# Two hybrid encoder layers on one core: cross attention in a written order, the rotation's tables at its end, state products from split operands, later transposes of x

## The chip, the core and the metric

The kernel runs on one core of one Trainium2 chip, as a single launch. The time is the device time of that launch in microseconds (us). Three runs of the kernel before took 2188.62, 2189.69 and 2190.12 us; the median, 2189.69 us, is the time that the change is compared with. One further execution was profiled; the profile shows when each instruction of each engine ran and what it waited for.

The engines carry these names: PE is TensorE (matrix products and transposes), PEld its loading of weights, DVE is VectorE, ACT is ScalarE, POOL is GpSimd, and SP is the queue of SyncE, from which all of this kernel's transfers are issued. An `L99` in a row of the profile is line 99 of the kernel; since most operations go through small helpers, many rows carry a helper's line, and the tile's name tells them apart.

## The reference

Two layers work on a residual stream x of 512 tokens and 1024 channels. Each layer has three branches on the same x, whose outputs are gated, summed, projected and normalised. All is float32.

- Branch A is a bidirectional state-space scan (SSD) with 4 groups g of 8 heads. A depthwise convolution over 5 tokens and SiLU make xs, B and C. The sequence is cut into 4 chunks of 128 tokens. For each group, chunk and direction there is a state: `states = einsum('bcqgn,bgrcq,bcqgrp->bcgrpn', bm, decay_states, xs)`, a product of B (128 tokens by 128) with the x of 8 heads (128 tokens by 512), weighted by a decay and by dt. Each state decays into the next chunk.
- Branch B is differential attention with rotary position, so it needs tables of cos and sin of position times frequency.
- Branch C is cross attention with 4 heads of 256 into 256 memory tokens: `s = q mk / 16; p = softmax(s); o = p mv`, and `y = o * silu(gate)`. The keys and values come from `mem @ w_mem_kv`, per layer.

Each branch is projected to 1024 channels and multiplied by a sigmoid gate computed from x.

## The kernel before

**Split products.** TensorE's fast float format (`F32R`) keeps fewer bits, so most operands are kept as a pair: `split(h, l, x)` writes h as a rounded copy (one instruction on ACT) and l = x - h (one subtraction on DVE, which needs h). `mm3` then does three matrix products: l by h, h by l, h by h. A plain `mm` on float32 tiles has no split.

**Units.** All weights come in units of 128 by 1024. A unit is loaded by a transfer (`wr`, 2 buffers), split (`wh`, `wl`, 3 buffers each; ACT and DVE), and used by one projection: 24 matrix products of 512 columns against xh and xl, into one of three PSUM banks `pj`. `emit` keeps loads and splits two units ahead of the unit that the plan has reached. The units for the memory's keys and values have 24 products of 256 columns.

**The plan.** `self.T(fn, unit)` appends to a plan; `emit` runs it in order and so gives every instruction a rank. A planner then orders each engine's instructions: it takes what is ready by its own costs, earliest rank first. Within `manual_schedule(engines={PE})` the order of TensorE alone is the written one; DVE, ACT and SP are still ordered by the planner. Each engine and each queue works through its list strictly in that order. `late(n)` changes the rank of what it encloses: with `-LN` the work counts as 300 places earlier.

**SSD stage (`ssd`).** TensorE's order is written out with `U` (a unit, and jobs placed between its two halves) and `J` (a job of its own). For group g there are the units B (`bu`), C (`cu`), four of x (`xu`), four of z (`zu`); `xturn(g, b)` transposes block b of x on TensorE once the convolution (ACT, four DVE steps `acc`, ACT into `xsC`) is done; `bturn` transposes B into `bT`. `expos(g, b)` loads decays by broadcast (`ab`, `eb`), clips them on DVE and exponentiates them on ACT into `m`. `block(g, b)` does the group's output for block b and reads `m` and the states `prev`. `states(g, part)` weights x on DVE (`xw`, line 518), multiplies `bT` by it on TensorE with a plain float32 `mm`, and adds the result to `prev`, for one chunk of each direction; there are 3 parts per group. `wu` projects the previous group, `gu` is one of 12 gate units, used to fill, whose result `tg` (2 buffers) goes to DRAM as `dgt` and is read back later.

**Cross stage (`cross`).** At its begin, in layer 0, the memory is loaded and split into `mhl` and `rope_tables` computes cos and sin with some 40 DVE steps in tiles `cw`. Then follow, head by head, q units (`qpart`), key units with a trip of the keys through DRAM (`mo`, `dkv`, `mkv`), gate units with the output of the head before (`opart`), the head's scores, softmax and transposes (`att`), and value units. The order of TensorE is the planner's here. In layer 1 the keys and values are made earlier, inside `wout` of layer 0. `branch_out` projects the branch.

Of the kernel before, what the change touches and what calls it, by code (L numbers as in the profile page):

```python
# [12 lines left out]
F32R = mybir.dt.float32r  # L13
# [38 lines left out]
class Net:  # L52
# [73 lines left out]

    def emit(self, look_raw=2, look=2):
# [110 lines left out]
    def rope_tables(self, sp, tag):  # L238
# [4 lines left out]
        t0, t1 = (self.t(sp, [P, 4, S], tag) for _ in range(2))  # L243
# [200 lines left out]
    def ssd(self, l):  # L444
# [66 lines left out]

        def states(g, part):

            sp = self.sp
            for d, c in ((0, part), (1, 3 - part)):
# [165 lines left out]
        def U(unit, *amid):  # L681
            gen, u = unit

            def f(wh, wl):
                g = gen(wh, wl)
                next(g, None)
                for fn, *args in amid:
                    fn(*args)
                next(g, None)
            self.T(f, u)  # L690

        def J(fn, *args):
            self.T(lambda: fn(*args))
# [50 lines left out]
        J(expos, 0, 0)  # L744
        U(gu())
        J(states, 0, 0)
        U(zu(0, 0), (states, 0, 1))
        for g in range(1, 4):
            p = g - 1
            U(bu(g))  # L750
            if g == 1:
                J(states, 0, 2)
# [6 lines left out]
            U(gu())  # L759
            J(block, p, 1)  # L760
            U(xu(g, 0), (bturn, g))
# [83 lines left out]
    def cross(self, l):  # L845
        nc = self.nc

        def begin():
            self.cp_ctx = ExitStack()
            cp = self.crp = self.cp_ctx.enter_context(self.tc.tile_pool(name="crossp", bufs=2, reuse_waits="tile"))  # L850
            if load is not None:
                load(cp, raw="cpp")
                self.rope_tables(cp, "cw")
# [3 lines left out]
        def fetch(i, h):  # L857
            def f():
                t = self.mkv[i] = self.t(self.crp, [P, 2, 2, M], f"mkv{i}", F32R)
# [3 lines left out]
        def qpart(h, i):  # L863
            def f(wh, wl):
                if i == 0:
                    self.cq = self.t(self.crp, [P, 2, 2, S], "cq", F32R)
                ps = self.proj(wh, wl)
                self.split(self.cq[:, 0, i, :], self.cq[:, 1, i, :], ps)
            return f

        def att(h):
            def f():
                cp = self.crp
                cq, mk = self.cq, self.mkv[0]
                cw = self.cw[h] = self.t(cp, [P, 2, 2, S], "cw", F32R)
                for qp in range(2):
                    ps = self.bank(self.pm, "pm")
                    for i in range(2):
                        q = slice((2 * qp + i) * P, (2 * qp + i + 1) * P)
                        for k in range(2):  # L880
                            self.mm3(ps[:, i * M:(i + 1) * M], cq[:, 0, k, q], cq[:, 1, k, q],
                                     mk[:, k, 0, :], mk[:, k, 1, :], k == 0, k == 1)
                    mx = self.t(cp, [P, 2], "cmx")
                    sm = self.t(cp, [P, 2], "csm")
                    psv = ps.rearrange("p (i m) -> p i m", i=2)
                    nc.vector.reduce_max(out=mx, in_=psv, axis=AX.X)
                    self.ts(mx, mx, -1.0 / 16.0, ALU.mult)
                    p = self.t(cp, [P, 2, M], "cpp")
                    for i in range(2):
                        self.act(p[:, i, :], psv[:, i, :], AF.Exp, scale=1.0 / 16.0, bias=mx[:, i:i + 1],  # L890
                                 accum_out=sm[:, i:i + 1])
                    nc.vector.reciprocal(out=sm, in_=sm)
                    for i in range(2):
                        self.ts(p[:, i, :], p[:, i, :], sm[:, i:i + 1], ALU.mult, 0.5, ALU.mult)
                    pt = self.bank(self.pt, "pt")
                    for k in range(2):
                        for i in range(2):
                            self.tr(pt[:, (2 * k + i) * P:(2 * k + i + 1) * P], p[:, i, k * P:(k + 1) * P])
                    q = slice(2 * qp * P, 2 * (qp + 1) * P)
                    self.split(cw[:, 0, :, q], cw[:, 1, :, q], pt.rearrange("p (k q) -> p k q", k=2))  # L900
            return f

        def opart(h, i):
            def f(wh, wl):
                cp, mv = self.crp, self.mkv[1]
                j = 2 * h + i
                ps = self.proj(wh, wl)
                th = self.t(cp, [P, S], "cth")
                self.act(th, ps, AF.Tanh, scale=0.5)
                self.stt(th, th, 1.0, ps, ALU.add, ALU.mult)  # L910
                po = self.bank(self.pm, "pm")
                for k in range(2):
                    e = slice(k * P, (k + 1) * P)
                    self.mm3(po, mv[:, i, 0, e], mv[:, i, 1, e], self.cw[h][:, 0, k, :], self.cw[h][:, 1, k, :],
                             k == 0, k == 1)
                self.tt(th, th, po, ALU.mult)
                self.split(self.cy[0][:, j, :], self.cy[1][:, j, :], th)
            return f
# [3 lines left out]
        def kv(i, h):  # L922
            if job is not None:
                for j in range(2):
                    self.T(*job(i, 2 * h + j))
            self.T(fetch(i, h))

        self.T(begin)
        for h in range(5):
            if h < 4:  # L930
                for i in range(2):
                    self.T(qpart(h, i), (l, UCQ + 2 * h + i))
                kv(0, h)
            if h:
                for i in range(2):
                    self.T(opart(h - 1, i), (l, UCG + 2 * (h - 1) + i))
            if h < 4:
                self.T(att(h))
                kv(1, h)
# [491 lines left out]
```

## Time and profile before

| | before |
|---|---|
| median of three runs | 2189.69 us |
| the profiled execution: its own time | 2190.09 us |
| its span, first to last instruction | 2188.3 us |
| granted TensorE clock, mean | 0.997 of full speed |
| PE busy | 2148.1 us, 98% of the span |
| DVE busy | 1546.6 us, 71% |
| ACT busy | 1152.1 us, 53% |
| instructions | 29240 |

Matrix products are pipelined and a row's duration reaches to the modelled end of the last one, so neighbouring rows overlap: what one costs in a full stream is the distance from its start to the next start. The "idle before" of a row is what the engine stood still ahead of it, and the name after the arrow is what ended that wait. In the first layer the SSD stage lasts to about 498 us, cross attention with its projection to 709; differential attention, the output projection and the next layer's keys and values follow to 1148. The second layer repeats that, with cross attention from 1635 to 1793 us.

### The profile page before, as it was taken

What the parts mean: (1) busy time and instruction counts of PE and PEld (TensorE: products, weight loads), DVE (VectorE), ACT (ScalarE), POOL (GpSimd) and SP (SyncE); (2) the same over time, 40 slices, a digit from 0 to 9 for tenths busy, and PEclk for the clock granted to TensorE, in tenths of its full rate; (3) what the DMA queues carried; (4) which work ended last, traced back from release to release, by engine and by line L of the source; (5) the groups of instructions that cost most, each with busy time, mean ns of one, the idle gap of its engine ahead of it and who ended that gap; (6) DMA issues with size and microseconds to landing.
All of it is one profiled execution on the core that took longest, in us unless ns stands there. A gap on an engine that the chain in (4) does not pass through costs nothing.

```text
span 2188.3 us, 29240 instructions
## 1 busy us (share of the span) xinstructions
PE 2148.1 (98%) x11122; PEld 1787.3 (82%) x11122; DVE 1546.6 (71%) x2404; ACT 1152.1 (53%) x2035; POOL 61.3 (3%) x38
## 2 busy tenths in 40 slices
PE   8999999999999999999999999999999999999998
PEld 6787878788888888887888777878788888888876
DVE  5677777869554788766566677878675547888667
ACT  5676757554432455543345676858533325555430
POOL 0010101010000000000000000101000000000000
PEclk9999999999999999999999999999999999999999
DMA  4654545454554433324564654545444334333253
GB/s 162 159 148 136 163 122 169 121 144 149 173 168 123 137 113 107 112 83 153 153 208 128 164 148 135 165 134 160 127 135 135 106 113 130 112 111 107 91 160 111
DMA packets 111984, 299.46 MB, mean 137 GB/s; under 512 B 12716, under 2 KB 13284, under 8 KB 111588
## 3 DMA queue, kind: packets, MB, share of 16 engines
q1 hardware_dynamic: 111844, 297.60, 46.0%
q8 instruction: 87, 1.43, 0.3%
q14 instruction: 53, 0.43, 0.1%
HBM read 257.16 MB, written 19.43 MB: 126 GB/s over the span
## 4 chain that ended last, share of the span: by engine, by line
PE 78%; DVE 9%; DMA 7%; ACT 2%; issue 2%; SPq 0%; DVEq 0%; ACTq 0%
PE pj L99 61%; PE pm L99 14%; DMA ab<-dab 4%; PE pt L107 2%; DVE acc L80 2%; DVE wl L77 2%; DMA wr<-wu 2%; DVE y L77 1%; DMA fth<-rd 1%; DVE eb L77 1%; ACT wh L87 1%; DVE ab L77 1%; ACT L87 1%; DVE y L80 1%; DMA mkv<-dkv 0%
## 5 line engine op out<-in xcount | busy, mean ns | idle before, releaser
L99 PE MATMUL pj<-xh,wl 128*128 128x512 f32 x1664 | 668.3, 402 | 0.2 <-DVE wl L77 0.2
L99 PE MATMUL pj<-xh,wh 128*128 128x512 f32 x1664 | 652.5, 393 | 8.1 <-ACT xh L87 6.0
L99 PE MATMUL pj<-xl,wh 128*128 128x512 f32 x1664 | 652.0, 392 | 0.0
L77 DVE TENSOR_TENSOR wl<-wr,wh 128x1024 fp32r<-128x1024 f32 x330 | 403.6, 1224 | 154.8 <-ACT wh L87 154.2
L87 ACT ACTIVATE wh<-wr 128x1024 fp32r<-128x1024 f32 x330 | 347.5, 1054 | 248.4 <-PE pj L99 169.5
L99 PEld LDWEIGHTS pj<-xh,wh 128*128 128x128 f32 x1664 | 314.0, 189 | 76.1 <-ACT xh L87 6.0
L99 PEld LDWEIGHTS pj<-xh,wl 128*128 128x128 f32 x1664 | 314.0, 189 | 70.8 <-issue 6.7
L99 PEld LDWEIGHTS pj<-xl,wh 128*128 128x128 f32 x1664 | 314.5, 189 | 65.0 <-issue 2.9
L87 ACT ACT_TABLE_LOAD x107 | 137.3, 1283 | 93.4 <-DVE ab L77 31.7
L87 ACT ACTIVATE ab<-ab,bias 128x128 f32<-128x128 f32 x512 | 161.3, 390 | 14.6 <-DVE ab L77 13.8
L80 DVE SCALAR_TENSOR_TENSOR acc<-pj,pr,acc 128x510 f32<-128x510 f32 (+1 forms) x192 | 142.2, 744 | 32.6 <-ACT acc L87 31.7
L77 DVE TENSOR_TENSOR ab<-ab,cst 128x1024 f32<-128x1024 f32 x64 | 78.2, 1223 | 72.9 <-DMA ab<-dab 72.8
L1059 DVE TENSOR_REDUCE fmx<-pm 128x1 f32<-128x512 f32 x128 | 85.0, 685 | 46.8 <-PE pm L99 46.8
L99 PE MATMUL pj<-yh,wl 128*128 128x512 f32 x256 | 106.1, 415 | 0.5 <-DVE mrg L77 0.5
L87 ACT ACTIVATE fpp<-pm,fmx 128x512 f32<-128x512 f32 x128 | 87.1, 685 | 33.8 <-DVE fmx L1059 33.8
L99 PE MATMUL pj<-dy,wh 128*128 128x512 f32 (+1 forms) x384 | 102.6, 356 | 0.9 <-DVE dy L77 0.9
L99 PE MATMUL pj<-yl,wh 128*128 128x512 f32 x256 | 100.2, 391 | 0.1
L99 PE MATMUL pj<-yh,wh 128*128 128x512 f32 x256 | 99.8, 390 | 0.0
L77 POOL TENSOR_TENSOR sqa<-sqa,sz 128x512 f32<-128x512 f32 x32 | 60.1, 1878 | 887.6 <-ACT sz L87 887.6
L99 PE MATMUL pj<-cy,wh 128*128 128x512 f32 x256 | 78.8, 389 | 0.0
L99 PEld LDWEIGHTS pj<-dy,wh 128*128 128x128 f32 x384 | 67.5, 188 | 13.2 <-DVE dy L77 2.1
L99 PE MATMUL pj<-wh,xl 128*128 128x256 f32 x256 | 73.3, 286 | 0.0
(274 smaller groups left out, 3309.2 us busy)
## 6 DMA issues: line engine op xcount, KB each, us to landing
wr<-wu SPq DMA_DIRECT2D x336, 512.0 KB, 3.7
ab<-dab SPq DMA_DIRECT2D x64, 512.0 KB, 5.6
eb<-deb SPq DMA_DIRECT2D x64, 256.0 KB, 5.9
mkv<-dkv SPq DMA_DIRECT2D x16, 512.0 KB, 4.1
rsw<-rx SPq DMA_DIRECT2D x64, 128.0 KB, 2.3
dy<-dy SPq DMA_DIRECT2D x32, 256.0 KB, 2.3
dgt<-tg SPq DMA_DIRECT2D x24, 256.0 KB, 3.9
dkv<-mo SPq DMA_DIRECT2D x16, 256.0 KB, 4.4
```

What stands on the lines that cost most here:

```text
L77: (eng or self.nc.vector).tensor_tensor(out=out, in0=a, in1=b, op=op)
L80: self.nc.vector.scalar_tensor_tensor(out=out, in0=a, scalar=s, in1=b, op0=op0, op1=op1)
L87: self.nc.scalar.activation(out=out, in_=a, func=f, **kw)
L99: self.nc.tensor.matmul(out=out, lhsT=a, rhs=b, start=first, stop=last)
L107: self.nc.tensor.transpose(out=out, in_=x, identity=self.ident)
L1059: nc.vector.tensor_reduce(out=mx[:, c:c + 1], in_=ps, axis=AX.X, op=ALU.min)
```

## The change

1. `states` multiplies split operands. `bturn` splits B's transpose into `bTh` and `bTl` instead of copying it. A new `weighted(g, part)` makes the weighted x (DVE, into a buffer of `y`), splits it into `xwh`, `xwl` (ACT, DVE), two buffers each, and its work is ranked 300 places earlier; it is called ahead of part 0 and, for the next part, at the end of each `states`. The product is an `mm3`.
2. In the written order of `ssd`, the transposes of x's blocks 0, 1 and 2 come later, `states` are moved to the middle of units, `block(0, 0)`'s first states come half a unit earlier, and one gate unit is taken out of group 3's round and put ahead of the first `states`. `tg` has one buffer.
3. `cross` is cut into steps q, k, v, s (scores and softmax), t (transposes), o (gate unit), p (product with the values), f (fetch), and TensorE follows a written string of steps, one for each layer.
4. `rope_tables` is called after the last step of layer 0's cross stage, just ahead of `branch_out`; its tiles take the space of `mhl`.

```diff
         def bturn(g):
...
-            G["bT", g] = self.t(self.sp, [P, S], "bT")
-            self.act(G["bT", g], pt)
+            G["bT", g] = [self.t(self.sp, [P, S], n, F32R) for n in ("bTh", "bTl")]
+            self.split(*G["bT", g], pt)
...
+        def ends(part):
+            return (0, part), (1, 3 - part)
+
+        def weighted(g, part):
+
+            with self.late(-LN):
+                for d, c in ends(part):
+                    hs = slice(d * 32 + g * 8, d * 32 + g * 8 + 8)
+                    xh, xl = G["xw", g, d] = [self.t(self.sp, [P, S], n, F32R, bufs=2) for n in ("xwh", "xwl")]
+                    xw = self.t(self.sp, [P, S], "y", bufs=2)
+                    self.tt(xw.rearrange("p (h e) -> p h e", h=8),
+                            G["xsT", g][:, c, :].rearrange("p (h e) -> p h e", h=8),
+                            bc(self.wst[:, c, hs, None], [P, 8, 64]), ALU.mult)
+                    self.split(xh, xl, xw)
+
         def states(g, part):
...
-                xw = self.t(sp, [P, 8, 64], "xw", bufs=2)
-                self.tt(xw, G["xsT", g][:, c, :].rearrange("p (h e) -> p h e", h=8),
-                        bc(self.wst[:, c, hs, None], [P, 8, 64]), ALU.mult)
                 ps = self.bank(self.pm, "pm")
-                self.mm(ps, G["bT", g][:, c * P:(c + 1) * P], xw)
+                self.mm3(ps, *(t[:, c * P:(c + 1) * P] for t in G["bT", g]), *G.pop(("xw", g, d)), True, True)
...
+            if part < 2:
+                weighted(g, part + 1)
...
-                o = self.t(self.sp, [P, S], "tg", bufs=2) if t is None else t()
+                o = self.t(self.sp, [P, S], "tg") if t is None else t()
...
         J(expos, 0, 0)
+        J(weighted, 0, 0)
         U(gu())
-        J(states, 0, 0)
+        U(gu(), (states, 0, 0))
         U(zu(0, 0), (states, 0, 1))
         for g in range(1, 4):
             p = g - 1
-            U(bu(g))
+            U(bu(g), *(((states, 0, 2),) if g == 1 else ()))
             if g == 1:
-                J(states, 0, 2)
                 U(zu(p, 1), (block, p, 0))
...
             U(cu(g))
-            U(gu())
-            J(block, p, 1)
-            U(xu(g, 0), (bturn, g))
+            if g < 3:
+                U(gu())
+                J(block, p, 1)
+            U(xu(g, 0), *(((block, p, 1),) if g == 3 else ()), (bturn, g))
             J(expos, p, 2)
             U(zu(p, 2), (within, g))
             U(xu(g, 1))
             J(block, p, 2)
+            U(zu(p, 3))
             J(xturn, g, 0)
-            U(zu(p, 3))
             J(expos, p, 3)
             U(xu(g, 2))
-            J(xturn, g, 1)
             J(block, p, 3)
-            U(xu(g, 3))
-            U(gu(), (xturn, g, 2))
+            U(xu(g, 3), (xturn, g, 1))
+            U(gu())
+            J(xturn, g, 2)
             U(wu(p, 0))
             J(xturn, g, 3)
+            J(weighted, g, 0)
             U(wu(p, 1))
             U(wu(p, 2), (states, g, 0))
-            J(states, g, 1)
-            U(wu(p, 3))
-            J(states, g, 2)
+            U(wu(p, 3), (states, g, 1))
             J(expos, g, 0)
-            U(zu(g, 0))
+            U(zu(g, 0), (states, g, 2))
...
     def cross(self, l):
...
-                self.rope_tables(cp, "cw")
...
+        order = ExitStack()
+        self.T(lambda: order.enter_context(self.tc.manual_schedule(engines={mybir.EngineType.PE})))
+        if l == 0:
+            steps = ("q00 q01 q10 q11 k00 k01 v00 v01 k10 k11 s00 v10 s01 v11 q20 t00 s10 q21 t01 s11 k20 k21 "
+                     "t10 o00 p00 t11 o01 p01 v20 v21 q30 s20 q31 s21 k30 k31 o10 t20 p10 o11 t21 p11 v30 v31 "
+                     "o20 s30 o21 s31 p20 o30 t30 p21 o31/t31 p30 p31")
+        else:
+            for i in range(2):
+                for h in range(2):
+                    mem(i, h, 1)
+            steps = ("q00 q01 q10 s00 q11 s01 q20 t00 q21 t01 s10 o00 s11 o01 t10 p00 q30 t11 p01 f02 f12 q31 s20 "
+                     "o10 s21 o11 t20 p10 o20 t21 p11 f03 f13 s30 o21 s31 p20 o30 t30 p21 o31/t31 p30 p31")
+        small = {"s": scores, "t": turn, "p": values}
...
+        self.T(order.close)
+        if l == 0:
+            self.T(lambda: self.rope_tables(self.crp, "mhl"))
         self.branch_out(l, lambda: self.crp, 2, UBC, lambda: self.cy, ("cth", "cpp", "cq", "cw"))
```

Each step's letter is followed by the head and by a number: the half of the head for q, k, v, o and p, the pair of query chunks for s and t. `o31/t31` puts the transposes between the halves of the unit. The instructions inside the steps are those of `qpart`, `att` and `opart` before.

More of the change, by code (lines that the diff above doesn't have):

```diff
@@ L125, in T, with unit, f, small @@
         self.plan.append((unit, fn))
+    def unit(self, unit, *amid):
+        gen, u = unit
+        def f(wh, wl):
+            g = gen(wh, wl)
+            next(g, None)
+            for fn, *args in amid:
+                fn(*args)
+            next(g, None)
+        self.T(f, u)
+    def small(self, fn, *args):
+        self.T(lambda: fn(*args))
     def emit(self, look_raw=2, look=2):
@@ L242, in rope_tables @@
         self.sin = self.t(self.cp, [P, S], "sin")
-        t0, t1 = (self.t(sp, [P, 4, S], tag) for _ in range(2))
+        t = self.t(sp, [P, 2, 4, S], tag, bufs=1)
+        t0, t1 = t[:, 0], t[:, 1]
         pi = t0[:, 0, :].bitcast(I32)
@@ L677, in ssd @@
         early = [gate(2, j) for j in range(KC)] + [gate(0, j) for j in range(4)]
[L681 to L693, printed above, removed]
+        U, J = self.unit, self.small
         def bu(g):
@@ L858, in f @@
             def f():
-                t = self.mkv[i] = self.t(self.crp, [P, 2, 2, M], f"mkv{i}", F32R)
+                t = self.mkv[i, h] = self.t(self.crp, [P, 2, 2, M], f"mkv{i}", F32R)
                 nc.sync.dma_start(out=t.bitcast(F32), in_=self.dk[i][2 * h:2 * h + 2].rearrange("j p s m -> p j s m"))
@@ L865, in f @@
                 if i == 0:
[L866 to L901, printed above, removed]
@@ new lines, in f, with scores @@
+                    self.cq[h] = self.t(self.crp, [P, 2, 2, S], "cq", F32R)
+                ps = yield from self.proj2(wh, wl)
+                self.split(self.cq[h][:, 0, i, :], self.cq[h][:, 1, i, :], ps)
+            return f, (l, UCQ + 2 * h + i)
+        def scores(h, qp):
+            cp = self.crp
+            cq, mk = self.cq[h], self.mkv[0, h]
+            if qp == 0:
+                self.cw[h] = self.t(cp, [P, 2, 2, S], "cw", F32R)
+            ps = self.bank(self.pm, "pm")
+            for i in range(2):
+                q = slice((2 * qp + i) * P, (2 * qp + i + 1) * P)
+                for k in range(2):
+                    self.mm3(ps[:, i * M:(i + 1) * M], cq[:, 0, k, q], cq[:, 1, k, q],
+                             mk[:, k, 0, :], mk[:, k, 1, :], k == 0, k == 1)
+            mx = self.t(cp, [P, 2], "cmx")
+            sm = self.t(cp, [P, 2], "csm")
+            psv = ps.rearrange("p (i m) -> p i m", i=2)
+            nc.vector.reduce_max(out=mx, in_=psv, axis=AX.X)
+            self.ts(mx, mx, -1.0 / 16.0, ALU.mult)
+            p = self.cp_[h, qp] = self.t(cp, [P, 2, M], "cpp")
+            for i in range(2):
+                self.act(p[:, i, :], psv[:, i, :], AF.Exp, scale=1.0 / 16.0, bias=mx[:, i:i + 1],
+                         accum_out=sm[:, i:i + 1])
+            nc.vector.reciprocal(out=sm, in_=sm)
+            for i in range(2):
+                self.ts(p[:, i, :], p[:, i, :], sm[:, i:i + 1], ALU.mult, 0.5, ALU.mult)
@@ L903, in opart, with turn @@
+        def turn(h, qp):
+            p, cw = self.cp_.pop((h, qp)), self.cw[h]
+            pt = self.bank(self.pt, "pt")
+            for k in range(2):
+                for i in range(2):
+                    self.tr(pt[:, (2 * k + i) * P:(2 * k + i + 1) * P], p[:, i, k * P:(k + 1) * P])
+            q = slice(2 * qp * P, 2 * (qp + 1) * P)
+            self.split(cw[:, 0, :, q], cw[:, 1, :, q], pt.rearrange("p (k q) -> p k q", k=2))
         def opart(h, i):
             def f(wh, wl):
-                cp, mv = self.crp, self.mkv[1]
@@ L906, in f @@
-                j = 2 * h + i
-                ps = self.proj(wh, wl)
-                th = self.t(cp, [P, S], "cth")
+                ps = yield from self.proj2(wh, wl)
+                th = self.cth[h, i] = self.t(self.crp, [P, S], "cth")
                 self.act(th, ps, AF.Tanh, scale=0.5)
                 self.stt(th, th, 1.0, ps, ALU.add, ALU.mult)
[L911 to L915, printed above, removed]
@@ L916, in f, with values @@
-                self.tt(th, th, po, ALU.mult)
-                self.split(self.cy[0][:, j, :], self.cy[1][:, j, :], th)
-            return f
+            return f, (l, UCG + 2 * h + i)
+        def values(h, i):
+            mv, th = self.mkv[1, h], self.cth.pop((h, i))
+            j = 2 * h + i
+            po = self.bank(self.pm, "pm")
+            for k in range(2):
+                e = slice(k * P, (k + 1) * P)
+                self.mm3(po, mv[:, i, 0, e], mv[:, i, 1, e], self.cw[h][:, 0, k, :], self.cw[h][:, 1, k, :],
+                         k == 0, k == 1)
+            self.tt(th, th, po, ALU.mult)
+            self.split(self.cy[0][:, j, :], self.cy[1][:, j, :], th)
@@ L920, in cross, with mem @@
         load, job = self.mem_kv(l) if l == 0 else (None, None)
-        def kv(i, h):
+        def mem(i, h, n):
             if job is not None:
-                for j in range(2):
-                    self.T(*job(i, 2 * h + j))
-            self.T(fetch(i, h))
-        self.T(begin)
[L929 to L939, printed above, removed]
+                fn, u = job(i, 2 * h + n)
+                self.T(fn, u)
+            if n:
+                self.T(fetch(i, h))
@@ new lines, in cross @@
+        U, J = self.unit, self.small
+        self.cq, self.cp_, self.cth = {}, {}, {}
+        self.T(begin)
+        order = ExitStack()
[5 more added lines that the diff above has]
+        else:
+            for i in range(2):
+                for h in range(2):
+                    mem(i, h, 1)
+            steps = ("q00 q01 q10 s00 q11 s01 q20 t00 q21 t01 s10 o00 s11 o01 t10 p00 q30 t11 p01 f02 f12 q31 s20 "
+                     "o10 s21 o11 t20 p10 o20 t21 p11 f03 f13 s30 o21 s31 p20 o30 t30 p21 o31/t31 p30 p31")
@@ new lines, in cross @@
+        small = {"s": scores, "t": turn, "p": values}
+        for step in steps.split():
+            step, *amid = step.split("/")
+            nm, h, i = step[0], int(step[1]), int(step[2])
+            if nm in small:
+                J(small[nm], h, i)
+            elif nm in "kv":
+                mem("kv".index(nm), h, i)
+            elif nm == "f":
+                mem(h, i, 1)
+            else:
+                U({"q": qpart, "o": opart}[nm](h, i), *((small[x[0]], int(x[1]), int(x[2])) for x in amid))
```

2 lines of the change are left out of this document (1 added, 1 removed).

## The prediction

> **What bounds the kernel now.** I read the page first (span, engines, chain), then the list of who waited for whom on TensorE, then the timeline at the places that the diff touches.
>
> ```profile
> span 2188.3 us, 29240 instructions
> PE 2148.1 (98%) x11122; PEld 1787.3 (82%) x11122; DVE 1546.6 (71%) x2404; ACT 1152.1 (53%) x2035; POOL 61.3 (3%) x38
> PE 78%; DVE 9%; DMA 7%; ACT 2%; issue 2%; SPq 0%; DVEq 0%; ACTq 0%
> ```
>
> ```profile
> PE pt L107 <- ACT xsC L87: 9.4, 7, 3.8
> PE pj L99 <- ACT xh L87: 6.0, 1, 6.0
> PE pm L99 <- DMA mkv<-dkv: 3.4, 2, 1.9
> PE pj L99 <- DVE wl L77: 3.0, 4, 1.7
> PE pj L99 <- ACT wh L87: 2.1, 1, 2.1
> PE pm L99 <- DVE m L77: 1.6, 2, 1.0
> PE pm L99 <- DVE prev L77: 1.5, 2, 0.8
> ...
> PE pj L99 <- DVE mrg L77: 0.5, 1, 0.5
> ```
>
> The columns of the second are total us, times and longest. TensorE is the bound: it makes up 78% of the chain and hardly stands still. So a change gains in two ways only: fewer array cycles, or less of these waits. 8.1 us of them (xh, the first wh) are the start, which is not touched. In reach are the transposes of x (9.4), m (1.6), prev (1.5) and one mrg (0.5) in the SSD stage, mkv (3.4) and part of wl (3.0) in cross attention.
>
> **States from split operands.** The product as it is:
>
> ```profile
> 87.82 1.88 PE L99 MATMUL pm<-xw,bT 128*128 128x512 f32 x4
> 89.13 0.79 PE L99 MATMUL pj<-xh,wl 128*128 128x512 f32 x1
> 89.77 0.40 PE L99 MATMUL pj<-xl,wh 128*128 128x512 f32 x1
> 90.00 0.40 PE L99 MATMUL pj<-xh,wh 128*128 128x512 f32 x1
> L99 PEld LDWEIGHTS pm<-xw,bT x96: 187/188/189, 87.6 to 1556.2; 128*128 128x128 f32 x96
> ```
>
> Two products leave four records. From the first of them to the second projection product are 1.95 us, in which one projection product runs too; that takes 0.23 (89.77 to 90.00). A float32 product is so (1.95 - 0.23) / 2 = 0.86 us. Three split products at 0.23 are 0.69. 96 records are 48 products: 48 x 0.17 = **8.2 us less**, straight off the bound. The three weight loads, 0.188 each, are shorter than the 0.23 that they run beside.
>
> What it costs elsewhere, by the same kinds of instruction on tiles of this size (nanoseconds: least, median, most):
>
> ```profile
> L87 ACT ACTIVATE cw<-pt x16: 574/598/601, 540.5 to 1741.0; 128x512 fp32r<-128x512 f32 x16
> L77 DVE TENSOR_TENSOR cw<-pt,cw x16: 683/691/692, 541.1 to 1741.6; 128x512 fp32r<-128x512 f32 x16
> ```
>
> Each weighted x gets an ACT copy (0.60) and a subtraction (0.69), and each B one subtraction: per layer 24 x 0.60 = 14.4 us on ACT and 28 x 0.69 = 19.3 us on DVE. They lie beside TensorE, unless the chain DVE, ACT, DVE is late. There is less room than DVE's 71% suggests (us, then busy of PE, PEld, DVE, ACT, POOL; clock; DMA):
>
> ```profile
> 313.00:343.00 30.00, 30.00 (x148) 24.57 (x147) 18.12 (x25) 12.77 (x19) 1.29 (x1) 1.00 0.44 121
> 392.00:420.00 28.00, 27.62 (x116) 20.70 (x114) 26.34 (x37) 19.06 (x37) 0.00 (x0) 1.00 0.53 147
> ```
>
> The second row is just where `states` and `wu` of group 3 run: DVE 94% busy, and six subtractions add 4.1 us to 26.3 of 28. It overflows by some 2.4 us into the stretch behind, which looks like the first row and has 12 us free. For parts 1 and 2 the copies also wait until TensorE has read the two buffers; from there to the next `states` are two half units, 5.5 us, against 2 x (0.60 + 0.69) = 2.6 of chain. The slack is 2.9 us, in a queue that is full. At best none of the 24 calls waits; at worst each finds the slack used up and then pays the subtractions, 1.4 us, 33 in all. I take 0.1 us for each, **2.5 us more**: `xw`, the nearest work, stands nowhere in the list of waits above.
>
> **The order of the SSD stage.** The largest wait:
>
> ```profile
> 166.71 1.23 DVE L77 TENSOR_TENSOR ab<-ab,cst 128x1024 f32<-128x1024 f32 x1 [4.73 <-DMA ab<-dab]
> 174.21 0.66 PE L107 MATMUL pt<-cst,xsC 128*128 128x128 f32 x4 [3.83 <-ACT xsC L87]
> 176.20 0.63 PE L99 MATMUL pj<-xh,wh 128*128 128x512 f32 x1
> 176.63 0.63 PE L99 MATMUL pj<-xh,wl 128*128 128x512 f32 x1
> 1295.62 0.66 PE L107 MATMUL pt<-cst,xsC 128*128 128x128 f32 x4 [0.68 <-ACT xsC L87]
> 1310.91 0.66 PE L107 MATMUL pt<-cst,xsC 128*128 128x128 f32 x4 [2.78 <-ACT xsC L87]
> 1312.52 0.63 PE L99 MATMUL pj<-xl,wh 128*128 128x512 f32 x1
> 1312.94 0.63 PE L99 MATMUL pj<-xh,wh 128*128 128x512 f32 x1
> ```
>
> DVE stood 4.73 us in front of a clip whose `ab` had not landed, and the convolution's steps stood behind it; so xsC came late. After either long wait, products come 0.43 us apart (176.20 to 176.63; 1312.52 to 1312.94) instead of 0.23; eight of them are 1.6 us more. These three waits are at blocks 1 and 2 of group 1, which the change puts later: block 1 by a `block` and half a unit, block 2 by half a unit (2.75 us); and the extra gate ahead of the first `states` gives DVE 5.5 us more before group 1. Block 2's 3.83 would be 1.1 left by the half unit alone, and the gate covers that. 7.3 of the 9.4 us lie there, plus 2 x 1.6 of slow clock: 10.5. The other 2.1 are waits for block 3, whose place stays. Once TensorE is early, block 3 of group 1 is the next to be late; I leave 2 us for it. The first `states` of prev get half a unit more than before on either side, far over their 0.8 each: 1.5 less. m and mrg stay. Sum **10.0 us less** (bounds: 0, and 9.4 + 3.2 + 1.6 + 1.5 + 0.5 = 16.2).
>
> The Trainium skill, "TensorE: Matmul & The Clock Gate", section "HAM oscillation", says that TensorE's clock halves after about 3.4 us without work. The first wait agrees with it; the second does not, since 2.78 us sufficed. By the rule the second clock loss, 1.6 us, would be no part of this wait's price, and the whole forecast would be 1.6 us higher.
>
> Group 3's round loses a gate, 5.5 us of cover, while DVE keeps its work; what that can bring is in a rival below. `tg` with one buffer needs each result landed before the next gate's end, 5.5 us on:
>
> ```profile
> DMA to landing us min/median/max: 2.0/3.9/6.7
> ```
>
> At the median it is hidden; at 6.7 ACT would stand about 2 us, which the two units of prepared weights cover. I take 0.
>
> **Cross attention.** In layer 0:
>
> ```profile
> 517.73 1.06 ACT L87 ACTIVATE wh<-wr 128x1024 fp32r<-128x1024 f32 x1
> 519.41 0.68 DVE L80 SCALAR_TENSOR_TENSOR cw<-cw 128x512 f32<-128x512 f32 x1
> 520.01 1.22 DVE L77 TENSOR_TENSOR wl<-wr,wh 128x1024 fp32r<-128x1024 f32 x1
> 521.28 0.39 PE L99 MATMUL pj<-wl,mhl 128*128 128x256 f32 x1 [1.71 <-DVE wl L77]
> 521.92 0.33 SPq L325 DMA_DIRECT2D dkv<-mo  x1
> 531.70 3.11 PE L99 MATMUL pm<-mkv,cq 128*128 128x256 f32 x24 [1.93 <-DMA mkv<-dkv]
> 534.65 0.40 PE L99 MATMUL pj<-xh,wl 128*128 128x512 f32 x1
> 1635.00:1793.00 158.00, 157.86 (x752) 130.66 (x751) 83.63 (x131) 52.22 (x89) 0.00 (x0) 1.00 0.37 117
> ```
>
> The rounded weights were there at 518.8, but DVE did the tables' steps (`cw`) first: the tables cost 1.7 us directly. The scores waited for the keys, 9.8 us after their write was issued. The written order puts four short units between k01 and s00, 4 x 2.95 (531.70 to 534.65) = 11.8 us, against 9.8 and two half-size splitting steps, under 1.3 by the rows above: just enough. Later heads have more. Eight short units now stand nearly in a row, each needing 1.06 + 1.22 us of splitting and a load within 2.95 us; the two units prepared ahead cover a lag of about 6 us. So of 3.4 + 1.7 + about 0.4 (the smaller wl and mhl) = 5.5 us I take **4.5 us less** (bounds 0 and 5.5). Layer 1 has PE busy 157.86 of 158: nothing to gain, and a written order can only lose there; all t, p steps have at least half a unit ahead of them, so I take 0.
>
> The tables' two largest groups of steps (busy us, mean ns), in 509 to 552:
>
> ```profile
> L80 DVE SCALAR_TENSOR_TENSOR cw<-cw 128x512 f32<-128x512 f32 x14 | 9.5, 685 | 0.0
> L84 DVE TENSOR_SCALAR cw<-cw 128x512 f32<-128x512 f32 x16 | 6.5, 421 | 0.1
> ```
>
> With some ten smaller steps that is over 20 us of DVE. It moves under the end of layer 0's cross stage and the eight 5.5 us units of `branch_out`, each with 2.6 of DVE work (1.22 and twice 0.69): 8 x 2.9 = 23 us are free there, and the space of `mhl` is free four units earlier still. cos is first wanted in the unit after that. Were that cover gone, 16 us and more would stand before the first rotation. I take **0.5 more**.
>
> **Sum**, against the profiled execution's own 2190.1 us (span 2188.3, 1.8 around it; the runs' median is 0.4 lower): -8.2 + 2.5 - 10.0 - 4.5 + 0.5 = -19.7, so about **2170 us**, own range 2163 to 2177.
>
> **Rivals.**
> - All waits in reach go and none comes: -8.2 - 16.2 - 5.5 = -29.9, 2160. For it: the gate's 5.5 us. Against it: block 3's place stays.
> - Given back: DVE's overflow moves the waits to `states`, to block 3 and to `wu`'s banks (the mrg wait shows that these can wait), 0.3 us on each of the 24 calls (7.2 for 2.5), and half of the 10.0 stays: 2170 + 4.7 + 5.0 = about 2180.
> - Slower: the split's copy stands on ACT behind an exponential whose `ab` is late, as DVE stood 4.73 us at 166.71. Where such a lag meets the 2.9 us slack, TensorE waits 4.7 - 2.9 = 1.8 at each of 24 calls: 43 us, so 2170 - 2.5 + 43 = about 2211. It decides from 22.2 / 24 = 0.9 us a call on. Against it: rank 300 places earlier, and ACT 68% busy there.
> - The change does not do what it says, because weight loads bind: 144 instead of 96 at 0.188 are 9.0 us more instead of 8.2 less, 2170 + 17.2 = 2187. Against it: the stream's 0.23 beside 0.19. The Trainium skill, "Perfetto Trace Analysis", section "Identifying the Most-Contended Engine", would judge TensorE by its weight loads; the trace speaks against that here.
>
> **Chances**: forecast 0.55, all gone 0.12, given back 0.19, slower 0.11, weight loads 0.03. Faster by over 0.2% (4.4 us, about what a measurement can tell from no change) means under 2185.3: 0.55 + 0.12 + most of 0.19, 0.84. Within: 0.06. Slower: 0.10. The range 2159 to 2186 leaves out the slower case and little else.
>
> **What would show it.** Two state products in 1.4 us instead of 1.7, and no wait for xw ahead of them; no xsC wait over 1 us and no stretch of 0.43 us after one; no mkv or wl wait in layer 0's cross attention; cos and sin written before the first rotation. I am wrong if TensorE's list of waits gets new entries of xw, prev or mrg that sum to over 10 us.

## The result and the profile after

Six runs of the changed kernel have a median of 2173.14 us (2170.19 to 2173.97). Against the kernel before, the ratio is 0.9920, with a 95% interval of 0.9909 to 0.9931: about 17 us, or 0.8%, faster. One of the six runs of the kernel before that were taken beside them lasted 4343.41 us; the ratio is of the others. The forecast was 2170 us. The profiled execution took 2173.1 us itself; the head of its page:

```profile
span 2171.4 us, 29416 instructions
PE 2136.6 (98%) x11170; PEld 1799.4 (83%) x11170; DVE 1581.6 (73%) x2460; ACT 1170.0 (54%) x2079; POOL 63.2 (3%) x38
PE 81%; DVE 8%; DMA 7%; issue 2%; ACT 1%; SPq 0%; DVEq 0%; ACTq 0%
```

TensorE is a larger part of the chain than before (81% for 78%), and its busy time fell by 11.5 us. Where the 16.9 us went by which the span is shorter is seen from the same three stretches of both kernels: to the last product of the first SSD stage, from there to the first product of `branch_out` (cross attention of layer 0), and what follows. The columns are us, then PE's busy time, clock, share of the DMA engines and GB/s. Before:

```profile
0.00:498.10 498.10, 483.27 (x2390) 1.00 0.51 146
498.10:665.90 167.80, 162.28 (x948) 1.00 0.54 167
665.90:2188.30 1522.40, 1502.58 (x7787) 1.00 0.44 130
```

After:

```profile
0.00:492.20 492.20, 478.59 (x2414) 0.99 0.51 148
492.20:654.30 162.10, 160.79 (x947) 1.00 0.56 172
654.30:2171.40 1517.10, 1497.26 (x7811) 1.00 0.44 131
```

So 5.9 us were won in layer 0's SSD stage with the start, 5.7 in its cross attention, and 5.3 in all that follows, which has the second SSD stage. TensorE's waits after:

```profile
PE pm L99 <- DVE m L77: 7.2, 2, 3.7
PE pj L99 <- ACT xh L87: 6.2, 1, 6.2
PE pj L99 <- ACT yh L87: 4.6, 2, 2.4
...
PE pm L99 <- DMA mkv<-dkv: 0.4, 1, 0.4
...
PE pm L99 <- DVE prev L77: 0.2, 1, 0.2
```

All of xsC (9.4 us) is gone, and prev (1.5), mrg (0.5) and mkv (3.4) nearly so. Two names are new or larger: m at block 3 of group 0 in each layer (7.2 for 1.6), and yh at the first `wu` behind the SSD stage's last block (4.6 for nothing). The states, by TensorE's timeline:

```profile
89.97 0.39 PE L99 MATMUL pm<-xwh,bTl 128*128 128x512 f32 x1
...
91.33 0.39 PE L99 MATMUL pj<-xh,wl 128*128 128x512 f32 x1
```

A pair is 91.33 - 89.97 = 1.36 us, for 1.72, and no xw stands in the list of waits. The two waits on m in the timeline, with what follows the second:

```profile
166.26 1.98 PE L99 MATMUL pm<-m,xsT 128*64 128x128 f32 x16 [3.71 <-DVE m L77]
1293.39 1.09 PE L99 MATMUL pm<-m,xsT 128*64 128x128 f32 x16 [3.52 <-DVE m L77]
...
1295.43 0.63 PE L99 MATMUL pj<-xh,wh 128*128 128x512 f32 x1
1295.86 0.63 PE L99 MATMUL pj<-xh,wl 128*128 128x512 f32 x1
```

Behind each, products stand 0.43 us apart, as they did behind the two long xsC waits of before. So the SSD stage stopped in other places, for nearly as long: m, yh and prev are 12.0 us now, where xsC, m, prev and mrg were 13.0.

### The profile page after: what moved, and what is told of

It reads as the page before. It is cut to its first block, busy times and chain, and to the rows that moved or that the text cites. A ratio compares the mean times of both kernels' runs of the same rounds, so it can differ in the third digit from the quotient of the medians.

```text
span 2171.4 us, 29416 instructions
## 1 busy us (share of the span) xinstructions
PE 2136.6 (98%) x11170; PEld 1799.4 (83%) x11170; DVE 1581.6 (73%) x2460; ACT 1170.0 (54%) x2079; POOL 63.2 (3%) x38
## 4 chain that ended last, share of the span: by engine, by line
PE 81%; DVE 8%; DMA 7%; issue 2%; ACT 1%; SPq 0%; DVEq 0%; ACTq 0%
PE pj L99 64%; PE pm L99 14%; DMA ab<-dab 4%; PE pt L107 2%; DVE wl L77 2%; DMA wr<-wu 2%; DVE ab L77 1%; DVE y L77 1%; DVE acc L80 1%; DMA fth<-rd 1%; DVE eb L77 1%; ACT wh L87 1%; DVE m L77 1%; DVE y L80 0%; PE pt L99 0%
## 5 line engine op out<-in xcount | busy, mean ns | idle before, releaser
L99 PE MATMUL pj<-yh,wl 128*128 128x512 f32 x256 | 101.7, 397 | 4.6 <-ACT yh L87 4.6
```

Source lines behind the costliest of these rows:

```text
L99: self.nc.tensor.matmul(out=out, lhsT=a, rhs=b, start=first, stop=last)
```

## The experiments

Two questions: what each part is worth, and why TensorE still waits in the SSD stage. All times below are medians, and all ratios are to the kernel before, run on the same chip beside each kernel. One thousandth of a ratio is 2.2 us.

In what follows, a lag is how late VectorE and ScalarE are when TensorE asks for their result.

**Plain states in the new order.** `G["bT", g]` is one tile, the weighted x isn't split:

```
-                    self.split(xh, xl, xw)
-                self.mm3(ps, *(t[:, c * P:(c + 1) * P] for t in G["bT", g]), *G.pop(("xw", g, d)), True, True)
+                self.mm(ps, G["bT", g][:, c * P:(c + 1) * P], G.pop(("xw", g, d)))
```

> The changed kernel, but its 48 state products are plain float32 again: the weighted x isn't split and B is turned into one tile. Order, gates and cross attention stay as changed. Theory A (the pairs of state products fell from 1.72 to 1.37 us because split operands cost 3 x 0.23 against 0.86 us, and the waits of 7.2 us on m and 4.6 us on yh come from the places that the order gives the blocks): 24 pairs x 0.35 us = 8.2 us slower than the changed kernel, about 2181 us, and the m and yh waits stay within 2 us of 7.2 and 4.6. Theory B (the two extra splits of ScalarE and VectorE at every call of states push the blocks behind): m and yh shrink below half, and the kernel is less than 4 us slower than the changed one, 2177 us or less.

Measured: 2178.52 us, ratio 0.9945 (0.9930 to 0.9960). That is 0.0025, 5.5 us, more than the changed kernel, between the two theories. Of TensorE's waits:

```profile
PE pj L99 <- ACT tg L87: 6.9, 2, 3.8
...
PE pj L99 <- ACT yh L87: 1.8, 2, 1.1
```

m no longer appears, but tg is there with 6.9 us: the unit `wu` behind the gate waits for the bank that ScalarE has yet to read. The longest stop of group 0 is about the same (3.0 and 3.8 for 3.7 and 3.5), some 15 us later. So the split doesn't make this lag; it only changes which instruction meets it. But yh gets shorter without the split, by 2.8 us. And the split products save 24 x 0.36 = 8.6 us of TensorE's time, of which 5.5 are left in the result: the split costs about 3 us elsewhere, for which yh is the one place that these traces show. The two intervals leave this difference uncertain by some 4 us.

**The old SSD order with split states**; states, block 1, the transposes of x and the gate of group 3 stand where they stood before.

```
-        U(gu(), (states, 0, 0))
+        J(states, 0, 0)
...
-            U(xu(g, 3), (xturn, g, 1))
-            U(gu())
-            J(xturn, g, 2)
+            U(xu(g, 3))
+            U(gu(), (xturn, g, 2))
...
```

> The changed kernel with the SSD order of before: states, transposes of x and block 1 stand where they stood, the gate of group 3's round is back; split states and cross attention stay as changed. Theory A (the order won little: the 9.4 us of waits on the transposes and 1.4 us on prev became 7.2 us on m and 4.6 us on yh, both with about 3 us of slow clock): the old waits return, m and yh fall below 2 us in all, and the time is within 3 us of the changed kernel, 2172 to 2177 us. Theory B (the forecast's: the order is worth 10 us by itself): 2183 us. A third outcome, that the old order with split states makes new waits at the states (the chain VectorE, ScalarE, VectorE stands right behind them there): over 2185 us, with PE waiting on xwl in most of the 24 calls.

Measured: 2190.88 us, ratio 1.0002 (0.9993 to 1.0012): the whole gain is gone, cross attention's included. The third outcome's time came, but not its reason. xwl isn't in the list, m is, at its head, and some of the old waits are back (xsC 7.7, prev 1.6):

```profile
PE pm L99 <- DVE m L77: 17.4, 4, 7.3
```

**The new cross attention alone** (states and SSD order of before), which completes the square. To the kernel before, only the diff's parts in `rope_tables` and `cross` are applied:

```
+        order = ExitStack()
+        self.T(lambda: order.enter_context(self.tc.manual_schedule(engines={mybir.EngineType.PE})))
...
+        if l == 0:
+            self.T(lambda: self.rope_tables(self.crp, "mhl"))
```

> The kernel before with the new cross attention and the rotation's tables at its end; the SSD part, with plain states and the old order, is that of before. Theory A (parts of the SSD part hang together: the split chain of VectorE and ScalarE makes TensorE wait where the old order leaves no work in front of it): the time is before's less the 3 to 6 us of cross attention, 2184 to 2187 us; then the split alone costs about 4 us in the old order (2190.9 with it) and saves 5.4 us in the new one. Theory B (the terms add, as the forecast took them): the old order costs 17.7 us with plain states as with split ones, so 2178.5 + 17.7 = 2196 us.

Measured: 2181.85 us, ratio 0.9971 (0.9959 to 0.9984). That is 0.0029, 6.3 us, by the new cross attention alone, near the 5.7 of the stretch in the changed kernel. With it in all four kernels, the ratios are:

| | plain states | split states |
|---|---|---|
| old order | 0.9971 | 1.0002 |
| new order | 0.9945 | 0.9920 |

The kernel of the old order with plain states also has the old two buffers of tg and makes its weighted x in place, so the differences that start from it include those. Each difference is uncertain by some 3 to 4 us. The terms don't add. Splitting costs 0.0031 (6.8 us) in the old order and saves 0.0025 (5.5 us) in the new. The new order saves 0.0026 (5.7 us) with plain states, where the intervals just touch, and 0.0082 (18 us) with split ones. Theory A holds in kind, with sizes off by 2 to 3 us.

**The old cross attention** (the planner's order, and the loop over heads with `qpart`, `kv`, `opart` and `att` in one piece), the tables still at its end:

```
-        order = ExitStack()
-        self.T(lambda: order.enter_context(self.tc.manual_schedule(engines={mybir.EngineType.PE})))
...
+        for h in range(5):
+            if h < 4:
+                for i in range(2):
+                    self.T(qpart(h, i), (l, UCQ + 2 * h + i))
...
```

> The changed kernel with the cross attention of before (TensorE's order left to the planner, att in one piece), the rotation's tables still behind it. Theory A (the written order saves the 4.5 us of waits that the old trace shows in layer 0, and about 1 us of shorter gaps): 5 to 6 us slower, about 2179 us, stage of cross attention in layer 0 at 210 to 211 us again. Theory B (the tables moved away from the start took the waits with them): within 2 us of the changed kernel, since the tables stay at the end here.

Measured: 2176.33 us, ratio 0.9932 (0.9917 to 0.9947), which overlaps with the changed kernel's. In its trace the stretch of cross attention in layer 0, from the last yh product to the first of cy, is 657.8 - 489.5 = 168.3 us:

```profile
L99 PE MATMUL pj<-yh,wh x32: 389/389/398, 464.1 to 489.5; 128*128 128x512 f32 x32
L99 PE MATMUL pj<-cy,wl x64: 389/389/393, 657.8 to 700.6; 128*128 128x512 f32 x64
```

That is before's length again (167.8; 162.1 changed), so the written order has the gain, not the tables' place. But the SSD stage ahead of it, the same in both, ended at 489.5 here and 492.2 there. Differences of 2 to 3 us, as between these two executions, may be why the medians show only half of the effect.

**The tables at the start of cross attention,** in the written order:

```
+                self.rope_tables(cp, "cw")
-            self.T(lambda: self.rope_tables(self.crp, "mhl"))
```

> The changed kernel with the written order of cross attention, but the rotation's tables worked out at its start again, in two tiles of cw. Theory A (the order carries the gain, the tables' place little): 1 to 3 us slower, 2174 to 2176 us, by the tables' VectorE and ScalarE work standing ahead of the first splits of q. Theory B (the tables' place carries the gain of 5.7 us): about 2179 us, with waits on cq or wl at the first score products.

Measured: 2170.07 us, ratio 0.9908 (0.9890 to 0.9926): not slower, though both theories had it slower. In its trace the stretch of cross attention, with the tables in it, lasts from 490.0 to 649.9, 159.9 us: the gain is there without the tables at the end. I tried it once more below.

**The gate back in group 3's round,** and not ahead of the first states.

```
-        U(gu())
         U(gu(), (states, 0, 0))
...
-            if g < 3:
-                U(gu())
-                J(block, p, 1)
-            U(xu(g, 0), *(((block, p, 1),) if g == 3 else ()), (bturn, g))
+            U(gu())
+            J(block, p, 1)
+            U(xu(g, 0), (bturn, g))
```

> The changed kernel with one gate unit moved back from the front of the first states to group 3's round, where it stood before. Theory A (the yh wait of 2.3 us at the last wu of each layer comes from the round that lost 6 us of TensorE work, so VectorE and ScalarE are 2.5 us later against TensorE): yh falls from 4.6 to under 1 us in both layers, 3 to 4 us faster, about 2169 us; but the m waits grow if the early gate gave group 0 its head start. Theory B (yh is late because the split states and transposes load VectorE): yh stays above 3 us and the time is within 1 us.

Measured: 2181.05 us, ratio 0.9961 (0.9946 to 0.9976), 9 us slower than the changed kernel. yh fell, from 4.6 to 2.4, but m rose from 7.2 in 2 to 12.3 in 4, and TensorE waited for the split of the weighted x (xwl, 1.9 us in 2), which isn't in the changed kernel's list:

```profile
PE pm L99 <- DVE m L77: 12.3, 4, 4.2
...
PE pj L99 <- ACT yh L87: 2.4, 2, 1.7
```

Theory A named the two effects, but had them the wrong way round in size. It is the only step of the new order that I took back alone, and it is worth half of what the order saves with split states.

**Block 3 later** than the last x unit, **the gate of the round g = 2 behind the last block,** and both:

```
-            J(block, p, 3)
             U(xu(g, 3), (xturn, g, 1))
+            J(block, p, 3)
```
```
-            if g < 3:
+            if g < 2:
                 U(gu())
...
+        U(gu())
         for j in range(4):
```

> The changed kernel with block 3 of a round written behind the unit xu(g,3) and not ahead of it: 5.5 us more of TensorE work before TensorE needs m. Theory A (the m wait of 3.7 and 3.5 us at block 3 of group 0 is a matter of place): both waits and the slow clock after them (8 products of 0.43 instead of 0.23 us, 1.6 us each) go, about 10 us faster, 2163 us; what remains is at most 1 us of transposes. Theory B (VectorE's loop over ab, 13.7 us a block, is as long as TensorE's and the delay only moves on): the wait comes back at a later block or at wu on yh, and the time is within 3 us of the changed kernel.

> The changed kernel with the gate unit of round 2 written behind the last block of the SSD stage, ahead of wu(3,0), which waits there 2.3 us on yh in both layers. Theory A (the wait needs only work to stand in front of it): yh falls from 4.6 to under 0.5 us and the time by 4 us, 2169 us, if round 2 has 5.8 us to spare. Theory B (round 2 needs its gate as cover): waits on m, xsC or prev of 3 us or more a layer appear in group 2's blocks, and the time is not below 2172 us.

> The changed kernel with both moves: block 3 behind xu(g,3), and the gate of round 2 behind the last block. Theory A (places, and the two add): 10 + 4 us, about 2159 us. Theory B (one VectorE loop under both): no more than the better of the two alone, 2165 us or above.

Measured: 2190.48 us (1.0012, 0.9999 to 1.0026), 2172.23 (0.9925, 0.9910 to 0.9939) and 2184.80 (0.9980, 0.9970 to 0.9990). The first is far worse than either theory had it. Its waits:

```profile
PE pj L99 <- ACT yh L87: 8.5, 7, 1.5
PE pt L107 <- ACT xsC L87: 6.4, 2, 3.3
...
PE pj L99 <- DVE yl L80: 3.4, 6, 0.6
```

The waits on m are gone and the lag is met by the transposes right behind (3.3 us). And block 3, later in every round, now gives `wu` its yh and yl too late in nearly every round; the wait for split weights (wl) rose too, from 0.9 to 5.6 us. With the gate moved, yh fell from 4.6 to below what the list shows, and in its place came, at the scores of group 3 (`within`), whose round had lost its cover:

```profile
PE pm L99 <- ACT cC L87: 4.8, 2, 2.5
```

4.6 us exchanged for 4.8. Both moves together lie between the two. These two moves chose which instruction meets a lag and did not shrink it. The early gate, which puts work of TensorE ahead of the first blocks, did more: without it m is 12.3 us, with it 7.2.

**The sum of ab in another tile.** What sets the lag? VectorE's timeline ahead of the wait at 162.5 us in the changed kernel:

```profile
143.29 0.68 DVE L77 TENSOR_TENSOR ab<-ab 128x512 f32<-128x512 f32 x1
143.89 0.74 DVE L80 SCALAR_TENSOR_TENSOR acc<-pj,pr,acc 128x511 f32<-128x511 f32 x1
144.55 0.68 DVE L77 TENSOR_TENSOR m<-ab,gs 128x512 f32<-128x512 f32 x1
...
150.88 1.23 DVE L77 TENSOR_TENSOR ab<-ab,cst 128x1024 f32<-128x1024 f32 x1 [1.88 <-DMA ab<-dab]
...
155.53 1.23 DVE L77 TENSOR_TENSOR ab<-ab,cst 128x1024 f32<-128x1024 f32 x1 [2.29 <-DMA ab<-dab]
...
163.56 1.29 DVE L77 TENSOR_TENSOR ab<-ab 128x512 f32<-128x512 f32 x2
...
165.43 1.28 DVE L77 TENSOR_TENSOR m<-ab,gs 128x512 f32<-128x512 f32 x2
```

and, by the view of the tile ab in 135 to 170 us:

```profile
DMA to landing us min/median/max: 5.4/5.9/6.4
```

The loads of the two clips that stood were issued at 145.29 and 149.07, just when the products `m<-ab,gs` begun at 144.55 and 148.32 were done. It is a loop: ab has two buffers; a buffer comes free when `m<-ab,gs` has read it; then the next load is issued and lands 5.9 us later; and VectorE, in strict order, stands before the clip of it (1.88 and 2.29 us), with all that is queued behind. Between the sum and the product that frees the buffer, the planner had put a step of the convolution (144.55 - 143.29 = 1.26 us). So:

```
-                self.tt(ab[:, 0], ab[:, 0], ab[:, 1], ALU.add)
                 m = self.t(sp, [P, 4, P], "m", bufs=3)
-                self.tt(m, ab[:, 0], G["gs", g], ALU.mult)
+                self.tt(m, ab[:, 0], ab[:, 1], ALU.add)
+                self.tt(m, m, G["gs", g], ALU.mult)
```

> The changed kernel, but in the steps ahead of a block the sum of the two halves of ab is written to m and not back to ab, so that a buffer of ab comes free one VectorE operation (0.68 us) earlier, for each of two heads a block, and its next load is issued earlier by that; no operation more or less. Theory A (the wait of 3.7 and 3.5 us at block 3 of group 0 is a lag of VectorE, which stood 10.6 us behind late loads of ab between 75 and 167 us): the lag shrinks by 1 to 3 us a layer, and with it some of the slow clock behind it; 2166 to 2171 us. Theory B (VectorE's own work sets the lag, the loads are late only because it is): the waits on m stay within 0.7 us of 7.2 and the time within 2 us of the changed kernel.

Measured: **2158.82 us, ratio 0.9859 (0.9844 to 0.9873)**: 0.0061, 13.4 us, faster than the changed kernel, and more than theory A had. TensorE's waits, and VectorE and TensorE at the same place:

```profile
PE pm L99 <- DVE m L77: 3.5, 2, 2.1
...
PE pj L99 <- ACT yh L87: 0.2, 1, 0.2
```

```profile
139.13 0.68 DVE L77 TENSOR_TENSOR m<-ab 128x512 f32<-128x512 f32 x1
...
147.19 1.22 DVE L77 TENSOR_TENSOR ab<-ab,cst 128x1024 f32<-128x1024 f32 x1
...
162.90 1.28 DVE L77 TENSOR_TENSOR m<-m,gs 128x512 f32<-128x512 f32 x2
```

```profile
163.73 1.09 PE L99 MATMUL pm<-m,xsT 128*64 128x128 f32 x16 [2.05 <-DVE m L77]
```

And the windows of 3.2 us behind this wait, in the changed kernel and here (the last three columns are clock, share of the DMA engines and GB/s):

```profile
168.10:171.30 3.20, 3.20 (x9) 2.48 (x8) 3.20 (x6) 1.06 (x1) 0.89 (x1) 0.50 0.78 193
```

```profile
165.60:168.80 3.20, 3.20 (x18) 2.65 (x17) 3.20 (x6) 1.60 (x2) 0.89 (x1) 1.00 0.98 334
```

VectorE gains more than the 0.68 us that I had counted for a turn, and the lead adds up: the clip of the changed kernel at 92.21 is at 91.73 here, the one at 140.83 at 136.79, and the one that stood at 150.88 is at 147.19, with nothing to wait for. Not all of that is the loop itself. In group 0's first block a buffer comes free 3.5 us earlier (its load is issued at 93.58, for 97.11), so its load and the next no longer go out together; the weights loaded right behind land sooner, ScalarE's wait for them falls from 5.29 to 3.58 us, and VectorE's wait on ScalarE behind it from 2.11 to 0.40. That is 1.7 us of the lead. VectorE's own stops in front of ab fell only from 10.6 to 9.6 us between 75 and 167 us: the next clip, at 151.87, still stood 3.46 us. The planner also put some steps of VectorE and some loads into another order, so how much the freed buffer does by itself is not separated. m falls by 3.7 us, yh by 4.4, and behind the wait of 2.05 us TensorE keeps its full clock, 18 products starting in 3.2 us for 9, which saves twice 1.6 more. That is 11.3 of the 13.4.

**The same edit in the kernel before:**

```
-                self.tt(ab[:, 0], ab[:, 0], ab[:, 1], ALU.add)
+                self.tt(m, ab[:, 0], ab[:, 1], ALU.add)
...
```

> The kernel before with the one edit of the last run: the sum of the halves of ab goes to m, so that a buffer of ab comes free 0.68 us earlier. Theory A (the lag of VectorE behind late loads of ab was there before too, and the 9.4 us on the transposes of x were where TensorE met it): the waits on xsC fall below 5 us, and the time by 5 to 12 us, to 2178 to 2184 us. Theory B (the lag of group 0's blocks came with the changed order and the split): the waits on xsC stay above 8 us and the time is within 2 us of the kernel before.

Measured: 2184.55 us, ratio 0.9975 (0.9962 to 0.9988), 5.5 us. xsC fell from 9.4 to 0.8, so the lag that my forecast read there was, as far as this edit singles it out, this loop's. The time follows less, since the states of the old order now stop on the weighted x, which nothing covers:

```profile
PE pm L99 <- DVE xw L77: 4.4, 4, 1.9
...
PE pt L107 <- ACT xsC L87: 0.8, 1, 0.8
```

With the edit in both kernels, the change is worth 0.9975 - 0.9859 = 0.0116, 25 us, instead of 17.

**The edit and the tables at the start,** in the changed kernel:

```
+                self.tt(m, ab[:, 0], ab[:, 1], ALU.add)
...
+                self.rope_tables(cp, "cw")
-            self.T(lambda: self.rope_tables(self.crp, "mhl"))
```

> The changed kernel with the sum of ab in m, and the rotation's tables at the start of cross attention as before, in two tiles of cw. The run with the tables at the start had 2170.1 us against 2173.1, but its waits on yh were 1.9 us shorter than in the changed kernel, in a part of the code that is the same in both. If the tables' place is worth the 3 us: about 2156 us. If the difference was the yh wait, which this kernel hardly has (0.2 us): 2158 to 2160 us, as with the sum of ab alone.

Measured: 2159.21 us, ratio 0.9859 (0.9840 to 0.9879), the same as the edit alone. The tables' place makes no difference that these runs can tell; the stretch of cross attention is 161.2 us long, with the tables in it.

## Why the prediction was right, and where it was not

The time was right to 3 us, but not all of it for the reasons given. Term by term, against the profiled executions and the square of four kernels:

| term | forecast | traces |
|---|---|---|
| split states, TensorE's time | -8.2 | -8.6 (24 pairs, 1.36 for 1.72) |
| chain of the split at the states | +2.5 | 0 there (no wait on xw); about +3 elsewhere (8.6 less the 5.5 of the square) |
| SSD order | -10.0 | about -6 (rest of the sum; -5.7 in the square, with plain states) |
| cross attention, layer 0 | -4.5 | -5.7 |
| the tables | +0.5 | 0, within what runs can tell |

The order came out some 4 us short, and the other terms made up 1.5 of that, so being 3 us off is in part luck. These are shares of one sum, not what a part is worth by itself: in the old order the split is a loss, and with split states the new order saves 18 us.

- **States.** The cost of the product was read rightly, and the three weight loads stayed hidden. The chain cost nothing at the states themselves; the weighted x is made one part ahead and ranked 300 places early, but whether that is why was not tried. But the extra work isn't free: in the new order it costs about 3 us, in yh as far as the traces show, and in the old order 6.8 us net, in m. My price of 0.1 us a call was put at the wrong place; that its size came out near is luck.
- **SSD order.** This is the step that was mis-sized, 10.0 us for about 6: "7.3 of the 9.4 us lie there, plus 2 x 1.6 of slow clock", with 2 us left for block 3. I took the wait as belonging to the transposes, and so as cured by putting them later. The row I quoted said otherwise: VectorE stood 4.73 us in front of a late ab. The later places of the transposes don't shorten that loop, so TensorE met the lag at the next thing it needed, m of block 3 (7.2 us, with both clock losses) and yh at the end (4.6). The 9.4 + 1.5 + 0.5 us that went and the 5.6 + 4.6 that came nearly cancel, though some 2.8 of the 4.6 go with the split and not with the order. This is the "given back" rival's mechanism, and at block 3 its place, and as it said little more than half of the 10.0 stayed; its time was too long mainly because it took 7.2 us for the chain, for about 3. My sign of being wrong, new waits on xw, prev or mrg of over 10 us, looked at the wrong tiles: 10.2 us came, on m and yh.
- **m stays** was wrong for the same reason (1.6 to 7.2).
- **The early gate** was rightly seen as cover for group 1: taking it back costs 9 us. That group 3's round lost it shows up in yh; putting it back there does not pay.
- **Cross attention.** Right in place: four short units between k01 and s00 were "just enough" (no wait there), mkv went from 3.4 to 0.4, wl from the stretch. The stretch is 159.9 to 163.4 us long in all eleven kernels with the written order, 166.9 to 168.3 in the three without. The gain passed its upper bound of 5.5 by 0.2, as the stretch shrank by more than its listed waits.
- **The tables** are covered by `branch_out`, as argued.
- **Rivals.** Weight loads don't bind. ScalarE did stand in front of the split's copies, 18.9 us in 8 stops, until TensorE had read the two buffers, but TensorE never waited there. The time of "all gone" was within reach, not by the order, but by freeing ab earlier: 2158.8 us with that edit beside its 2160, though waits of 3.5 us on m were still there.
- What remains open: why the old order with split states has m waits of up to 7.3 us. Its trace points at the same loop: VectorE stood 4.64 us in front of a late ab until 147.47, and TensorE's wait of 6.85 us on m ended at 151.18. But that order was not run with the sum of ab in m, which would have told.

## What to carry to other kernels

A wait in the list names what TensorE asked for first, not what is late. Follow it back to the engine that stood still, and if a loop over few buffers with a transfer in it is behind, moving the asker may only rename the wait: stops of 3 to 4 us were called xsC, m and tg here. Look at which instruction frees the buffer and bring that one forward. And price parts of a change in the order they are combined: here one of them alone is a loss.

## What the runs showed of the hardware

TensorE's stretch of 0.43 us a product doesn't go by the length of one stop. All single stops of 3.0 us and more in the SSD stages, behind the first 60 us, were followed by it, mostly for some eight products. Of the shorter ones, 2.05 us (above) was not; but in the kernel with both moves a stop of 1.88 us, which ended at 180.40 and had 11 us of work at full clock ahead of it, was: from 181.36 to 183.92 products begin 0.42 to 0.43 us apart. And the kernel with the gate moved has both, at the same instruction of the two layers:

```profile
343.21 2.08 PE L99 MATMUL pm<-cC,bC 128*128 128x128 f32 x8 [2.29 <-ACT cC L87]
...
345.51 0.63 PE L99 MATMUL pj<-xl,wh 128*128 128x512 f32 x1
345.93 0.56 PE L99 MATMUL pj<-xh,wh 128*128 128x512 f32 x1
...
1470.12 1.16 PE L99 MATMUL pm<-cC,bC 128*128 128x128 f32 x8 [2.53 <-ACT cC L87]
...
1471.35 0.39 PE L99 MATMUL pj<-xl,wh 128*128 128x512 f32 x1
1471.58 0.39 PE L99 MATMUL pj<-xh,wh 128*128 128x512 f32 x1
```

The shorter stop is followed by two products 0.42 us apart, the longer one by none. And in the kernel with block 3 later, two stops that sum to 1.92 us were enough:

```profile
294.16 0.50 PE L99 MATMUL pj<-yh,wl 128*128 128x512 f32 x1 [1.34 <-ACT yh L87]
...
295.47 0.50 PE L99 MATMUL pj<-yl,wh 128*128 128x512 f32 x1 [0.58 <-DVE yl L80]
...
297.86 0.63 PE L99 MATMUL pj<-yh,wh 128*128 128x512 f32 x1
298.29 0.63 PE L99 MATMUL pj<-yl,wh 128*128 128x512 f32 x1
```

So it looks like a measure of recent work rather than of one stop; what it is measured over was not tried. The Trainium skill, "TensorE: Matmul & The Clock Gate", section "HAM oscillation", gives about 3.4 us without work for it; the stops of 1.88 and 2.29 us and the pair of 1.92 had less and were followed by it.
